# Layer norm on ScalarE, output projection over token tiles of both halves in turn, first FFN pair's second product copied by ScalarE

## The chip, the cores and the metric

One core of a Trainium2 chip runs the kernel. Its engines work side by side, each through its own queue in order: TensorE (PE, matmuls, with PEld for its weight loads), VectorE (DVE), ScalarE (ACT), GpSimd (POOL), and SyncE (SP), which here issues the transfers. Matmul results stand in PSUM, in banks of 128 x 512 float32; everything else on the chip is in SBUF. The metric is the device time of one execution in microseconds (us).

## The reference

A residual stream `x` of 1024 tokens by 1024 goes through two layers. Layer 0 mixes dilated window attention and latent attention, layer 1 is differential attention; both end in an output projection. Then each layer does the same:

```python
x = layer_norm(ALPHA * x + y, ln_mix_g[i], ln_mix_b[i])     # y: output projection of the mixer
f = conv_ffn(x, ffn_w_gate[i], ffn_w_up[i], ffn_conv_w[i], ffn_conv_b[i], ffn_w_down[i])
x = layer_norm(ALPHA * x + f, ln_ffn_g[i], ln_ffn_b[i])
x = x + jax.nn.sigmoid(x @ ple_w_gate[i]) * (p[i] @ ple_w_proj[i])
```

`layer_norm` takes mean and variance over the 1024 columns of a token, and then scales by a gain and adds a bias. `conv_ffn` is a gated FFN of width 2816 with a convolution of three tokens on the gate.

## The kernel before

Tokens lie in eight tiles of 128; the host has put the even tokens into tiles 0 to 3 (the first half) and the odd ones into tiles 4 to 7 (the second half). Every float32 matmul is done as three: each operand is split into a high part (a rounded copy, mostly by ACT or POOL) and a low part (the rest, mostly by DVE), and `mm3` multiplies high by high, high by low and low by high.

**Output projection** (`out_proj`, L1052). For each tile t: SP loads the residual row; `load(t + 1)` fetches and splits the next tile's mixer output (`mhl`); `linear(t)` runs 48 matmuls into a pair of banks, and DVE adds the residual (L1077). Then the tile before is put away (`xt.put(t - 1)`), this one is normed (`ln`), and SP stores it (`xmid`). For the last tile the order is: first FFN weights (`early`), linear, norm, and then the putting away of tile 6; tile 7 is put away by the FFN (`late`). Norm and split of one tile thus stand beside the linear of the next.

**Layer norm** (`LN`, L876) has two parts. `stats`: two `bn_stats` of 512 columns and one `bn_aggr` on DVE, then two small steps on POOL for the reciprocal root (L895, L896). `apply`: DVE subtracts the mean and scales (L901), DVE multiplies by the gain (L902), and POOL adds the bias, or DVE where the argument `last` is true (L903; the last two tiles of an output projection, and all of the embedding stage). The first DVE instruction is pinned: it stays behind all that was written before it for DVE. Other instructions may stand in another order on an engine than in the text; the order is fixed when the kernel is built.

**Splits for the FFN** (`XSeven.put`, L338). The FFN's two products work by a scheme with seven products in place of eight on halves of tokens and halves of the contraction: `b00` and `b10` are the first half's rows, `t1` and `b11` come from the second half with the first half's values subtracted, and `t2`, `t3`, `t4` are made of both at the end (`finish`). PE transposes the tile into two banks; for tiles 0 to 3 ACT copies four high parts and DVE makes four low ones; for tiles 4 to 7 there are twelve operations on DVE and five on ACT, and DVE and ACT take turns on a bank. Tile t of the second half needs tile t - 4.

**FFN** (`ffn`, L1222). For each of 22 weight blocks m, seven products of 12 matmuls, in the order a00, s2, s3, s1, a01, a11, s4. The first pair (m = 0, 1) runs in another order, a00 and a01 first, then s1, s4, s2, s3, a11, since these need the second half later (`go_ahead`, `ahead`). a00 and s2 share a pair of banks (`pa`), of which there are two; the other products take one of four banks (`pb`). `read` adds the products up: `m` is a copy of a00 by ACT, `u2 = m + s2` is one DVE add that reads the bank (through the helper line L1167), and `u3`, `c01` and the rest are built on `u2`.

**Embedding stage** (`Embedding`, L1391). The same `LN` is used on the FFN's result; the norm of tile t + 2 is written ahead of the linear of tile t. The norms of tiles 0 and 1 lie inside the last group of the down projection.

Buffers: 36 units of 4 KB a partition (`unit`) hold rows, weights and splits; `b00` and `b10` take eight of them, the second half's splits twelve.

Of the kernel before, what the change touches and what calls it, by code (L numbers as in the profile page):

```python
# [11 lines left out]
AF = mybir.ActivationFunctionType  # L12
ALU = mybir.AluOpType
AX = mybir.AxisListType

P = 128
NT = 8
# [3 lines left out]
LN_EPS = 1e-5  # L21
# [10 lines left out]
def tile_hybrid_encoder(  # L32
# [32 lines left out]
    nc = tc.nc  # L65
# [8 lines left out]
    def nm(s):  # L74
        count[0] += 1
        return f"{s}_{count[0]}"

    def unit(s, shape, dt=F32):
        return up.tile(shape, dt, tag="u", name=nm(s))
# [29 lines left out]
    def small(s, shape, dt=F32, bufs=6):  # L109
        return sm.tile(shape, dt, tag=s, name=nm(s), bufs=bufs)  # L110
# [4 lines left out]
    def mid2(s, shape, dt=F32):  # L115
        return sm.tile(shape, dt, tag="mid2", name=nm(s), bufs=4)
# [4 lines left out]
    def bank(s):  # L121
        return ps.tile([P, 512], F32, tag="b", name=nm(s), bufs=4)

    def banks2(s):
        return ps.tile([P, 1024], F32, tag="s", name=nm(s), bufs=2)

    def f32(ap):
        return ap.bitcast(F32)
# [28 lines left out]
    def mm3(o, lh, ll, rh, rl, start, stop):  # L157
        nc.tensor.matmul(o, lhsT=lh, rhs=rh, start=start, stop=False)  # L158
        nc.tensor.matmul(o, lhsT=lh, rhs=rl, start=False, stop=False)  # L159
        nc.tensor.matmul(o, lhsT=ll, rhs=rh, start=False, stop=stop)  # L160
# [116 lines left out]
    class XTok:  # L277
# [26 lines left out]
        def load(self, t):  # L304
            self.raw[t] = unit("x0r", [P, NK, P])
            nc.sync.dma_start(out=self.raw[t], in_=xT_in[t])
# [10 lines left out]
    def add(o, a, b, op=ALU.add, eng=None):  # L317
        (eng or nc.vector).tensor_tensor(f32(o), f32(a), f32(b), op=op)
# [557 lines left out]
    class LN:  # L876
# [7 lines left out]
            self.apply(x, self.stats(x), last)  # L884

        def stats(self, x, pin=True):
            st = small("st", [P, 2, 6], bufs=3)
            mv = small("mv", [P, 2], bufs=3)
            rs = small("rs", [P, 1], bufs=3)
            for i in range(2):  # L890
                ins = nc.vector.bn_stats(out=st[:, i, :], in_=x[:, i * 512:i * 512 + 512])
                if pin:
                    tc.keep_in_program_order(ins)
            nc.vector.bn_aggr(out=mv, in_=st)
            nc.gpsimd.tensor_scalar(rs, mv[:, 1:2], 1.0, LN_EPS, op0=ALU.mult, op1=ALU.add)  # L895
            nc.gpsimd.tensor_tensor(rs, rs, mhalf, op=ALU.pow)  # L896
            return mv, rs

        def apply(self, x, stats, last=False):
            mv, rs = stats  # L900
            nc.vector.tensor_scalar(x, x, mv[:, 0:1], rs, op0=ALU.subtract, op1=ALU.mult)  # L901
            nc.vector.tensor_tensor(x, x, self.g, op=ALU.mult)  # L902
            (nc.vector if last else nc.gpsimd).tensor_tensor(x, x, self.b, op=ALU.add)  # L903

# [115 lines left out]
    def mixer_c(xt, late):  # L1020
        new_region(3)
        oT2 = big("oT2", [P, 2, 1024])
        last = {}

        def sink(i):
            def f(oT):
                if i < 7:
                    nc.sync.dma_start(out=mix[1][i], in_=oT)
                last["oT"] = oT
            return f  # L1030
        blk = [Block64(xt, w_c[i], False) for i in range(8)]
        blk[0].load(True)
        for t in range(NT):
            blk[0].project(t, 2)
            if t == 1:
                late()
        blk[0].keys(NT - 2)
        items, plan = [], Plan()
        for i in range(8):
            sti = {"sink": sink(i), "oT": oT2[:, i % 2, :] if i < 7 else unit("oT", [P, 1024])}  # L1040
            items += [ItemC(blk[i], t, sti) for t in range(NT)]
            if i < 7:
                blk[i + 1].plan(plan, 8 * i - 1, 1)
            else:
                w, mt = last_plan(plan, 1, 56, 63)
        plan.add(-1, "first", lambda: blk[0].keys(NT - 1))
        plan.add(-1, "last", lambda: blk[1].load(True), lambda: blk[1].project(0))
        pipeline(items, plan)
        return w, mt, last["oT"]


    def out_proj(i, w, mt, oT, xsrc, xt, early):  # L1052

        ln = LN(ln_mg[i], ln_mb[i])
        xns, m = [], mt.m

        def load(t):
            if t < NT:
                if t not in m:
                    mt.seven(t)  # L1060
                mt.last(t, oT)

        def residual(t):
            xns.append(unit("xn", [P, 1024]))
            nc.sync.dma_start(out=xns[t], in_=xsrc[t])

        def linear(t, beside=None):

            xr, mt_ = xns[t], m.pop(t)
            po = banks2("po")  # L1070
            for k in range(NK):
                if k == NK // 2 and beside:
                    beside()
                for n in range(2):
                    sl = slice(512 * n, 512 * n + 512)
                    mm3(po[:, sl], *mt_[k], w[k][0][:, sl], w[k][1][:, sl], k == 0, k == NK - 1)
            nc.vector.scalar_tensor_tensor(xr, xr, ALPHA, po, op0=ALU.mult, op1=ALU.add)  # L1077

        load(0)
        for t in range(NT):  # L1080
            residual(t)
            load(t + 1)
            if t < NT - 1:
                linear(t)
            else:
                early(0)
                linear(t, lambda: early(1))
                ln(xns[t], True)
                nc.sync.dma_start(out=xmid[i][t], in_=xns[t])
            if t:  # L1090
                xt.put(t - 1, xns[t - 1])
            if t < NT - 1:
                ln(xns[t], t == NT - 2)
                nc.sync.dma_start(out=xmid[i][t], in_=xns[t])
        return lambda: xt.put(NT - 1, xns[NT - 1])


    class Weights:
# [37 lines left out]
    class Products:  # L1136
# [27 lines left out]
        def read(self):  # L1164

            def plus(o, a, name):
                nc.vector.tensor_tensor(o, a, self.o[name], op=ALU.add)  # L1167
            out = []
            had = set(x for x, _ in self.sums)
            for name, need in list(self.sums):  # L1170
                before = {"m": (), "u2": ("m",), "u3": ("u2",), "c11": ("u3",), "c00": ("m",) if self.ahead else ("u2",), "c10": ("u3", "c11"), "k5": (),
                          "c01": ("c11",)}[name]
                if any(x not in self.o for x in need) or any(x in had for x in before):
                    continue
                if name == "m":
                    self.m = mid2("m", [P, 512])
                    nc.scalar.copy(self.m, self.o["a00"])
                elif name == "u2":
                    u = unit("u", [P, 2, 512])
                    self.u2, self.u3 = u[:, 0, :], u[:, 1, :]  # L1180
                    plus(self.u2, self.m, "s2")
                elif name == "u3":
                    plus(self.u3, self.u2, "s3")
                elif name == "k5":
                    self.c11 = mid2("c11", [P, 512])
                    nc.scalar.copy(self.c11, self.o["s1"])
                elif name == "c11" and self.ahead:
                    nc.gpsimd.tensor_tensor(self.u2, self.u2, self.c11, op=ALU.add)
                    nc.vector.tensor_tensor(self.c11, self.u3, self.c11, op=ALU.add)
                elif name == "c11":  # L1190
                    self.c11 = mid2("c11", [P, 512])
                    plus(self.c11, self.u3, "s1")
                    plus(self.u2, self.u2, "s1")
                elif name == "c00":
                    if self.c00 is None:
                        self.c00 = self.m
                    plus(self.c00, self.m, "a01")
                elif name == "c10":
                    plus(self.u3, self.u3, "a11")
                    self.c10 = self.u3  # L1200
                elif name == "c01":
                    plus(self.u2, self.u2, "s4")
                    self.c01 = self.u2
                had.discard(name)
                out.append(name)
            self.sums = [x for x in self.sums if x[0] in had]
            return out
# [254 lines left out]
    xt = XTok()  # L1462
    for i in range(2):
        if i == 0:
            w, mt, oT = mixer_ab(xt)
        else:
            tc.keep_in_program_order(nc.scalar.preload_act_table_set("natural_log_exp_and_others"))
            w, mt, oT = mixer_c(xt, late)
# [3 lines left out]
        if i == 0:  # L1472
            xt = XTok()
# [102 lines left out]
```

## Time and profile before

| | |
|---|---|
| median of 3 runs | 3108.19 us (3105.83 to 3110.84) |
| the profiled execution | 3106.23 us |
| its span | 3104.4 us |
| output projection of layer 0, first to last matmul | 703.2 to 799.6 us |
| its FFN's first product | from 799.5 us |
| last matmul of the output projection of layer 1 | begins at 2314.6 us |
| granted PE clock over the span | 0.994 |

In a row of the profile stand line, engine, operation, output and inputs by name, their shapes, the count, and then busy time and mean of one in ns, and idle time of the engine just before with what ended it (`<-`). A helper's operations all carry the helper's line: L141 is every low part, L1167 every add of `plus`, L163 every transpose. Rows of the order of time have the start and the duration first. A busy PE need not be a PE at its peak: matmuls overlap in the pipeline.

### The profile page before, as it was taken

The page shows a single profiled execution, that of the slowest core. Times are in us where ns is not written, and L with a number is a line of the kernel's source. Part 1 is how long each engine was busy: PE and PEld are TensorE (multiplying, and loading weights), DVE is VectorE, ACT ScalarE, POOL GpSimd, SP SyncE. Part 2 cuts the span into 40 slices and gives each one's busy share as a digit, 9 for nine tenths or more (in the row PEclk, how much of TensorE's full clock was granted, in tenths as well). Part 3 has the DMA queues.
Part 4 walks back from the last instruction along what each step waited for, and adds up shares of the span by engine and source line. Part 5 has one row for each costly group of instructions (what it writes and reads, how often), then busy time and mean ns, then how long its engine had stood idle before and what let it go on. Part 6 is the DMA issues. An engine that isn't in the chain of part 4 may idle for free.

```text
span 3104.4 us, 43067 instructions
## 1 busy us (share of the span) xinstructions
PE 3008.3 (97%) x15720; PEld 2582.7 (83%) x15720; DVE 2280.5 (73%) x3890; ACT 1186.8 (38%) x2538; POOL 1022.9 (33%) x1536
## 2 busy tenths in 40 slices
PE   8999999999899999999999999999998999999999
PEld 7888989887678888888888999998776888878887
DVE  6666487876898887766638777777679888877764
ACT  5555477761232222101225555555413222211111
POOL 4444534333222221101225555554223222211112
PEclk9999999999999999999999999999999999999999
DMA  3000100033222222623111000002431222243321
GB/s 121 28 28 24 33 28 8 25 126 126 85 82 82 82 82 93 220 95 109 55 59 36 32 28 28 28 24 77 156 107 68 82 82 82 82 176 136 103 77 65
DMA packets 89251, 237.52 MB, mean 77 GB/s; under 512 B 9040, under 2 KB 32720, under 8 KB 89040
## 3 DMA queue, kind: packets, MB, share of 16 engines
q1 hardware_dynamic: 89040, 234.76, 22.0%
q8 instruction: 125, 2.05, 0.3%
q14 instruction: 86, 0.70, 0.1%
HBM read 179.15 MB, written 55.57 MB: 76 GB/s over the span
## 4 chain that ended last, share of the span: by engine, by line
PE 79%; DVE 10%; DMA 3%; ACT 2%; issue 2%; POOL 2%; SPq 0%; DVEq 0%; ACTq 0%; POOLq 0%
PE pb L159 6%; PE pb L160 6%; PE pb L158 6%; PE xt L163 5%; PE pd L158 4%; PE pd L159 4%; PE pd L160 4%; PE pp L158 4%; PE pp L160 4%; PE pp L159 4%; PE s L587 4%; PE pa L158 2%; PE pa L160 2%; PE pa L159 2%; PE pg L158 2%
## 5 line engine op out<-in xcount | busy, mean ns | idle before, releaser
L141 DVE TENSOR_TENSOR ptl<-xt,pth 128x512 fp32r<-128x512 f32 (+2 forms) x384 | 239.6, 652 | 60.3 <-ACT pth L398 43.6
L158 PE MATMUL pd<-dh,dh 128*128 128x512 f32 x704 | 274.8, 390 | 3.0 <-DVE xn L1378 2.9
L1378 DVE TENSOR_TENSOR xn<-xn,pd 128x512 f32<-128x512 f32 x320 | 212.5, 683 | 87.9 <-PE pd L160 87.2
L158 PE MATMUL pp<-wh,xth 128*128 128x384 f32 x768 | 266.2, 347 | 9.7 <-ACT wh L145 7.3
L159 PE MATMUL pd<-dl,dh 128*128 128x512 f32 x704 | 274.1, 389 | 0.3 <-DVE dl L141 0.3
L160 PE MATMUL pd<-dh,dl 128*128 128x512 f32 x704 | 273.3, 389 | 0.0
L159 PE MATMUL pp<-wl,xth 128*128 128x384 f32 x768 | 259.0, 337 | 1.9 <-DVE wl L148 1.7
L160 PE MATMUL pp<-wh,xtl 128*128 128x384 f32 x768 | 258.0, 336 | 0.0
L439 ACT ACTIVATE e<-s,nmx 128x1024 f32<-128x1024 f32 x192 | 214.5, 1119 | 81.8 <-DVE nmx L837 59.0
L163 PE MATMUL xt<-ident,e 128*128 128x128 f32 x1440 | 198.8, 275 | 9.9 <-POOL e L739 3.0
L324 ACT CAST w<-ws 128x512 fp32r<-128x512 f32 x132 | 81.3, 621 | 331.6 <-PE pb L160 285.9
L158 PE MATMUL pb<-xt,w 128*128 128x512 f32 x528 | 207.1, 392 | 0.0
L159 PE MATMUL pb<-xt,w 128*128 128x512 f32 x528 | 206.9, 392 | 0.0
L160 PE MATMUL pb<-xt,w 128*128 128x512 f32 x528 | 206.7, 392 | 0.0
L163 PEld LDWEIGHTS xt<-ident,e 128*128 128x128 f32 x1440 | 164.1, 141 | 30.6 <-ACT sq L869 5.8
L138 POOL TENSOR_SCALAR w<-ws 128x512 fp32r<-128x512 f32 x44 | 32.5, 741 | 469.3 <-PE pa L160 419.0
L324 ACT CAST dh<-dr 128x1024 fp32r<-128x1024 f32 x44 | 46.1, 1052 | 335.8 <-DMA dr<-gated 202.1
L141 DVE TENSOR_TENSOR w<-ws,w 128x512 fp32r<-128x512 f32 x176 | 161.0, 918 | 4.5 <-ACT w L324 2.2
L138 POOL TENSOR_SCALAR dh<-dr 128x1024 fp32r<-128x1024 f32 x44 | 46.2, 1052 | 356.1 <-PE pd L159 168.5
L158 PEld LDWEIGHTS pd<-dh,dh 128*128 128x128 f32 x704 | 132.2, 188 | 32.7 <-DVE xn L1378 5.1
L158 PEld LDWEIGHTS pp<-wh,xth 128*128 128x128 f32 x768 | 144.6, 188 | 15.2 <-ACT wh L145 8.1
L159 PEld LDWEIGHTS pd<-dl,dh 128*128 128x128 f32 x704 | 132.2, 188 | 27.7 <-DVE dl L141 0.7
(281 smaller groups left out, 8732.4 us busy)
## 6 DMA issues: line engine op xcount, KB each, us to landing
wf<-in_w_gate_dram SPq DMA_DIRECT2D x44, 512.0 KB, 3.8
wf<-in_w_up_dram SPq DMA_DIRECT2D x44, 512.0 KB, 4.1
gated<-c SPq DMA_DIRECT2D x44, 512.0 KB, 2.8
dr<-in_w_down_dram SPq DMA_DIRECT2D x44, 512.0 KB, 3.2
dr<-gated SPq DMA_DIRECT2D x44, 512.0 KB, 3.5
wr<-in_w_c_dram SPq DMA_DIRECT2D x32, 384.0 KB, 3.3
pes<-peo SPq DMA_DIRECT2D x64, 128.0 KB, 1.9
xmid<-xn SPq DMA_DIRECT2D x16, 512.0 KB, 2.8
```

Source lines behind the costliest of these rows:

```text
L138: nc.gpsimd.tensor_scalar(o, i, 1.0, 1.0, op0=ALU.mult, op1=ALU.mult)
L141: nc.vector.tensor_tensor(lo, src, f32(hi), op=ALU.subtract)
L158: nc.tensor.matmul(o, lhsT=lh, rhs=rh, start=start, stop=False)
L159: nc.tensor.matmul(o, lhsT=lh, rhs=rl, start=False, stop=False)
L160: nc.tensor.matmul(o, lhsT=ll, rhs=rh, start=False, stop=stop)
L163: nc.tensor.transpose(o, in_=i, identity=ident)
L324: nc.scalar.copy(h, v)
L439: nc.scalar.activation(dst, s, AF.Exp, bias=negmax, scale=1.0, accum_out=l)
L587: nc.tensor.matmul(s[:, kh * 512:kh * 512 + 512], lhsT=qt[:, hl, i, :], rhs=self.ks[kh][:, j, :], start=hl == 0, stop=hl == 1)
L1378: nc.vector.tensor_tensor(xns[t][:, sl], xns[t][:, sl], po, op=ALU.add)
```

## The change

Layer norm: the sum over a row comes from an ACT copy in place with its accumulator (pinned on ACT); POOL makes minus the mean over 32; two ACT squares of 512 columns, with that as bias and a scale of 1/32, write to a PSUM bank that nobody reads and give the variance by their accumulators; POOL takes two small steps to the reciprocal root and a third to mean times root; ACT scales and shifts the row. DVE keeps the multiplication by the gain, and POOL or DVE the bias as before.

Output projection: the tiles come in the order 0, 4, 1, 5, 2, 6, 3, 7.

FFN, first pair only: ACT copies s2 out of its bank, and DVE adds `m` to it in SBUF.

```diff
--- before.py
+++ after.py
@@ -884,21 +884,24 @@
             self.apply(x, self.stats(x), last)
 
         def stats(self, x, pin=True):
-            st = small("st", [P, 2, 6], bufs=3)
-            mv = small("mv", [P, 2], bufs=3)
-            rs = small("rs", [P, 1], bufs=3)
+
+            st = small("st", [P, 6], bufs=3)
+            sums, sq, nm, rs, nmr = st[:, 0:1], st[:, 1:3], st[:, 3:4], st[:, 4:5], st[:, 5:6]
+            ins = nc.scalar.activation(x, x, AF.Identity, accum_out=sums)
+            if pin:
+                tc.keep_in_program_order(ins)
+            nc.gpsimd.tensor_scalar(nm, sums, -1.0 / (1024 * 32), 1.0, op0=ALU.mult, op1=ALU.mult)
             for i in range(2):
-                ins = nc.vector.bn_stats(out=st[:, i, :], in_=x[:, i * 512:i * 512 + 512])
-                if pin:
-                    tc.keep_in_program_order(ins)
-            nc.vector.bn_aggr(out=mv, in_=st)
-            nc.gpsimd.tensor_scalar(rs, mv[:, 1:2], 1.0, LN_EPS, op0=ALU.mult, op1=ALU.add)
+                nc.scalar.activation(bank("sq"), x[:, i * 512:i * 512 + 512], AF.Square, bias=nm, scale=1.0 / 32,
+                                     accum_out=sq[:, i:i + 1])
+            nc.gpsimd.tensor_scalar(rs, sq[:, 0:1], sq[:, 1:2], LN_EPS, op0=ALU.add, op1=ALU.add)
             nc.gpsimd.tensor_tensor(rs, rs, mhalf, op=ALU.pow)
-            return mv, rs
+            nc.gpsimd.tensor_scalar(nmr, rs, nm, 32.0, op0=ALU.mult, op1=ALU.mult)
+            return nmr, rs
 
         def apply(self, x, stats, last=False):
-            mv, rs = stats
-            nc.vector.tensor_scalar(x, x, mv[:, 0:1], rs, op0=ALU.subtract, op1=ALU.mult)
+            nmr, rs = stats
+            nc.scalar.activation(x, x, AF.Identity, bias=nmr, scale=rs)
             nc.vector.tensor_tensor(x, x, self.g, op=ALU.mult)
             (nc.vector if last else nc.gpsimd).tensor_tensor(x, x, self.b, op=ALU.add)
 
@@ -1052,16 +1055,18 @@
     def out_proj(i, w, mt, oT, xsrc, xt, early):
 
         ln = LN(ln_mg[i], ln_mb[i])
-        xns, m = [], mt.m
-
-        def load(t):
-            if t < NT:
+        xns, m = {}, mt.m
+        turn = [4 * (n % 2) + n // 2 for n in range(NT)]
+
+        def load(n):
+            if n < NT:
+                t = turn[n]
                 if t not in m:
                     mt.seven(t)
                 mt.last(t, oT)
 
         def residual(t):
-            xns.append(unit("xn", [P, 1024]))
+            xns[t] = unit("xn", [P, 1024])
             nc.sync.dma_start(out=xns[t], in_=xsrc[t])
 
         def linear(t, beside=None):
@@ -1077,22 +1082,22 @@
             nc.vector.scalar_tensor_tensor(xr, xr, ALPHA, po, op0=ALU.mult, op1=ALU.add)
 
         load(0)
-        for t in range(NT):
+        for n, t in enumerate(turn):
             residual(t)
-            load(t + 1)
-            if t < NT - 1:
+            load(n + 1)
+            if n < NT - 1:
                 linear(t)
             else:
                 early(0)
                 linear(t, lambda: early(1))
                 ln(xns[t], True)
                 nc.sync.dma_start(out=xmid[i][t], in_=xns[t])
-            if t:
-                xt.put(t - 1, xns[t - 1])
-            if t < NT - 1:
-                ln(xns[t], t == NT - 2)
+            if n:
+                xt.put(turn[n - 1], xns[turn[n - 1]])
+            if n < NT - 1:
+                ln(xns[t], n == NT - 2)
                 nc.sync.dma_start(out=xmid[i][t], in_=xns[t])
-        return lambda: xt.put(NT - 1, xns[NT - 1])
+        return lambda: xt.put(turn[-1], xns[turn[-1]])
 
 
     class Weights:
@@ -1178,7 +1183,11 @@
                 elif name == "u2":
                     u = unit("u", [P, 2, 512])
                     self.u2, self.u3 = u[:, 0, :], u[:, 1, :]
-                    plus(self.u2, self.m, "s2")
+                    if self.ahead:
+                        nc.scalar.copy(self.u2, self.o["s2"])
+                        add(self.u2, self.u2, self.m)
+                    else:
+                        plus(self.u2, self.m, "s2")
                 elif name == "u3":
                     plus(self.u3, self.u2, "s3")
                 elif name == "k5":
```

## The prediction

> **What bounds the kernel now.** I read the page first, then the busy time by stretches, then the list of who waited for whom, and at last the order of instructions where PE waits.
>
> ```profile
> span 3104.4 us, 43067 instructions
> ...
> PE 3008.3 (97%) x15720; PEld 2582.7 (83%) x15720; DVE 2280.5 (73%) x3890; ACT 1186.8 (38%) x2538; POOL 1022.9 (33%) x1536
> ```
>
> PE stands idle for 3104.4 - 3008.3 = 96.1 us in all. Work taken off another engine can only win where PE waits for that engine, so the question is where the 96 us lie. These are stretches of the first layer, one row that the second layer gives for the same place, and one of the embedding stage (us, then busy time and count of PE, PEld, DVE, ACT, POOL, granted clock, DMA):
>
> ```profile
> core 0: us, PE busy (x) PEld busy (x) DVE busy (x) ACT busy (x) POOL busy (x), PEclk, DMA share, GB/s
> ...
> 800.00:848.00 48.00, 36.84 (x159) 28.83 (x157) 44.82 (x67) 16.31 (x28) 13.25 (x11) 0.93 0.19 66
> 848.00:860.00 12.00, 10.72 (x36) 8.43 (x37) 11.42 (x17) 5.36 (x7) 3.26 (x3) 0.71 0.00 1
> 860.00:896.00 36.00, 33.40 (x146) 26.84 (x145) 35.71 (x51) 11.73 (x17) 13.53 (x12) 1.00 0.29 100
> 896.00:1240.00 344.00, 344.00 (x1504) 280.66 (x1503) 275.17 (x390) 100.18 (x143) 88.46 (x85) 1.00 0.23 83
> 1480.00:1560.00 80.00, 79.91 (x396) 66.62 (x395) 54.48 (x79) 18.61 (x34) 17.82 (x23) 1.00 0.17 60
> 2315.00:2411.00 96.00, 81.36 (x340) 64.52 (x339) 91.98 (x132) 33.45 (x51) 30.00 (x25) 0.93 0.20 70
> ```
>
> From 800 to 896 us, the turn from the output projection to the FFN, DVE is busy 44.82 + 11.42 + 35.71 = 91.95 of 96 us and PE 80.96; the second layer has 91.98 and 81.36. After 896 PE is never idle (344 of 344, 344 / 1504 = 0.229 us a matmul), and so it is in the embedding stage (79.91 of 80). So two stretches of 96 us are DVE's, and nearly all the rest in reach of this change is PE's. PE's waits over the whole span say the same:
>
> ```profile
> PE pa L158 <- DVE u L1167: 18.3, 2, 9.2
> ...
> PE xt L163 <- POOL xn L903: 4.9, 4, 1.8
> PE pb L158 <- DVE t L318: 4.0, 2, 2.0
> ...
> PE pb L158 <- DVE u L1167: 2.8, 2, 1.4
> ...
> PE xt L163 <- DVE xn L903: 2.4, 4, 0.7
> PE pa L158 <- ACT m L1177: 2.2, 2, 1.2
> ```
>
> They come to 34.6 us, 17.3 a layer. Slow matmuls after the longest wait cost more: 848 to 860 has 36 in 10.72 us, 10.72 - 36 x 0.229 = 2.5 us too long, at a clock of 0.71. So about 20 us a layer, 40 in all, is the ceiling of this change.
>
> **Layer norm, off DVE.** The prices on DVE and POOL now:
>
> ```profile
> L891 DVE BATCH_NORM_STATS2 st<-xn 128x6 f32<-128x512 f32 x64 | 41.4, 680 | 0.2
> ...
> L902 DVE TENSOR_TENSOR xn<-xn,lngb 128x1024 f32<-128x1024 f32 x32 | 39.1, 1222 | 0.6
> ...
> L901 DVE TENSOR_SCALAR xn<-xn,mv,rs 128x1024 f32<-128x1024 f32 x32 | 26.6, 831 | 26.0 <-POOL rs L896 26.0
> L894 DVE BATCH_NORM_AGGREGATE mv<-st 128x2 f32<-128x12 f32 x2 | 0.4, 190 | 0.0
> L903 POOL TENSOR_TENSOR xn<-xn,lngb 128x1024 f32<-128x1024 f32 x12 | 29.5, 2458 | 26.7 <-DVE xn L902 26.7
> ...
> L896 POOL TENSOR_TENSOR rs<-rs,mhalf 128x1 f32<-128x1 f32 x32 | 17.5, 548 | 2.7
> L895 POOL TENSOR_SCALAR rs<-mv 128x1 f32<-128x1 f32 x32 | 8.0, 248 | 156.7 <-DVE mv L894 156.1
> ```
>
> DVE loses 2 x 0.68 + 0.19 + 0.83 = 2.38 us a token tile, 76 us over 32 tiles. Of these only the tiles normed inside the DVE-bound stretch count: the last two of each output projection, 4.8 us a layer. ACT takes the work over; these are the nearest rows:
>
> ```profile
> L439 ACT ACTIVATE e<-s,nmx 128x1024 f32<-128x1024 f32 x192 | 214.5, 1119 | 81.8 <-DVE nmx L837 59.0 <-DVE nmx L735 22.6
> ...
> L324 ACT CAST w<-ws 128x512 fp32r<-128x512 f32 x132 | 81.3, 621 | 331.6 <-PE pb L160 285.9 <-DVE c L1242 33.4 <-DVE ws L318 10.8
> ...
> L324 ACT CAST dh<-dr 128x1024 fp32r<-128x1024 f32 x44 | 46.1, 1052 | 335.8 <-DMA dr<-gated 202.1 <-DVE xn L1378 113.4 <-PE pd L160 15.7
> ...
> L439 ACT ACTIVATION_READ_ACCUMULATOR e<-s,nmx 128x1 f32 x192 | 37.5, 195 | 0.0
> ...
> L1234 ACT ACTIVATE c<-c,convt 128x512 f32<-128x512 f32 x24 | 19.6, 816 | 92.6 <-DVE c L1167 74.9 <-DVE c L1189 11.2 <-DVE xt L141 6.6
> ```
>
> The sum: 1.05 to 1.12 plus a read of 0.20. Two squares of 512: between the plain 0.62 and 0.82 (bias and scale both from a tile), I take 0.7 for the single bias, plus 0.20 each: 1.8. The scaling, 1024 elements with both: 0.82 + (1.05 - 0.62) = 1.25. ACT gains 4.3 us a tile; at 16.31 busy of 48 it has room. The chain from residual to normed row is now 2 x 0.68 + 0.19 + 0.25 + 0.55 + 0.83 = 3.2 us before the multiply by the gain. After: 1.3 + 0.25 (mean) + 1.8 + 0.25 + 0.55 + 0.25 (three POOL steps) + 1.25 = 5.65, and two more changes of engine. I take **2.5 us longer**; the bounds are 2.0 (squares at 0.62, steps hidden) and 3.5 (POOL steps stretched beside DVE).
>
> On this cost the Trainium skill bears (ScalarE: Activation LUTs, Rules for kernel authors): adds and multiplies belong on VectorE and not on ScalarE. The trace agrees on the single price, 0.83 us on DVE against 1.05 for a plain pass on ACT; by that rule alone the edit would only lengthen the chain, which is the last rival below.
>
> **What the longer chain meets.** The splits of tiles 3, 4 and 5 in the first output projection begin at these transposes (PE), and the norms of tiles 4 and 5 at these statistics (DVE); the last row is the end of tile 4's norm (POOL):
>
> ```profile
> 762.15 1.03 PE L163 MATMUL xt<-ident,xn 128*128 128x128 f32 x8
> 773.93 1.04 PE L163 MATMUL xt<-ident,xn 128*128 128x128 f32 x8
> 787.85 1.09 PE L163 MATMUL xt<-ident,xn 128*128 128x128 f32 x8 [1.76 <-POOL xn L903]
> ```
>
> ```profile
> 765.02 1.28 DVE L891 BATCH_NORM_STATS2 st<-xn 128x6 f32<-128x512 f32 x2
> ...
> 780.09 1.28 DVE L891 BATCH_NORM_STATS2 st<-xn 128x6 f32<-128x512 f32 x2
> ```
>
> ```profile
> 769.64 2.41 POOL L903 TENSOR_TENSOR xn<-xn,lngb 128x1024 f32<-128x1024 f32 x1 [2.19 <-DVE xn L902]
> ```
>
> The statistics are pinned behind the split of the tile before, which waits for that tile's norm: a loop. For a tile of the first half (light split) it runs 762.15 to 769.64 + 2.41 = 772.05, 9.9 us; for one of the second half (heavy split) 773.93 to 787.85, 13.9. PE's own period is 773.93 - 762.15 = 11.8. So a light loop has 1.9 us to spare and a heavy one makes PE wait. With 2.5 more, less some 0.4 and 1.1 because the sum now follows ACT's last copy and not DVE's last operation behind it, a light loop takes 12.0 and a heavy one 15.3 or a little less. In turn 0, 4, 1, 5, 2, 6, 3, 7 three heavy loops lie in the projection (before: two), each 2.5 to 3.5 late, and the waits of 4.9 + 2.4 become about 3 us more a layer: the last linear ends some **2.6 us later**.
>
> **Token tiles in turn.** The price of one operation of a split, from DVE's groups of 786 to 896 us:
>
> ```profile
> L318 DVE TENSOR_TENSOR t<-xt,t 128x256 f32<-128x256 f32 x6 | 2.5, 411 | 0.0
> ```
>
> A heavy split has 12 such operations, 4.9 us; a light one 4, 1.7. Before, tiles 5, 6 and 7 are split after 786 us; after the change 6, 3 and 7. DVE is spared 4.9 - 1.7 = **3.2 us** a layer there, and the heavy ones go to where DVE has room. The price: the first FFN product reads the first half's rows and now needs tile 3, the last but one, where before it needed nothing but weights. PE then waits some 3 us after the last linear; those four products before hid a later wait, so I put this at nothing, up to 3 if DVE isn't ahead by then. Loads and stores only change order; the twelve buffers of the second half are taken three tiles sooner, so SP's loads of the next tile wait for a buffer that the middle of each linear gives back, half a period of 11.8 us ahead of need.
>
> **The first pair's copy.** This is the longest wait:
>
> ```profile
> 849.28 0.77 PE L158 MATMUL pa<-xb,w 128*128 128x512 f32 x1 [9.17 <-DVE u L1167]
> ```
>
> ```profile
> 845.93 1.28 DVE L141 TENSOR_TENSOR w<-wf,w 128x512 fp32r<-128x512 f32 x2
> ...
> 848.45 1.28 DVE L1167 TENSOR_TENSOR u<-m,pa 128x512 f32<-128x512 f32 x2
> ```
>
> PE stops because the bank of the second product is read at 848.45 only. ACT could read it some 10 us sooner. But the weights that PE needs next are split by DVE until 847.2, and the next two products want banks that still wait for DVE's add into u3. So alone this frees 849.28 - 847.2 = 2 us a layer at most; DVE's own add stays (0.68 us). I count 0.5, since it decides only where DVE has come first.
>
> On the slow matmuls the Trainium skill says (TensorE: Matmul & The Clock Gate, Part 1) that an idle window of about 3.4 us halves the clock and a busy one restores it. The clock of 0.71 after 9.17 us agrees; by that rule the 2.5 us come back whole if the wait falls under 3.4.
>
> **The sum.** DVE is spared 4.8 + 3.2 = 8.0 us a layer in the stretch that it bounds. The last norm, from which the heavy split of tile 7 and all of the second half follow, comes later. Now:
>
> ```profile
> 799.24 0.39 PE L160 MATMUL po<-woh,mhl 128*128 128x512 f32 x1
> ```
>
> ```profile
> 801.74 1.20 DVE L1077 SCALAR_TENSOR_TENSOR xn<-xn,po 128x1024 f32<-128x1024 f32 x1
> ...
> 808.66 1.22 DVE L903 TENSOR_TENSOR xn<-xn,lngb 128x1024 f32<-128x1024 f32 x1
> ```
>
> From the last linear's end at 799.63 to the norm's end at 809.88 are 10.25 us, though its parts need 1.20 + 3.2 + 2 x 1.22 = 6.85: 3.4 us are DVE's queue. After, the linear is 2.6 later and the chain 2.5 longer, but most of that queue is gone: about 2 us later. 8.0 - 2.0 + 0.5 = 6.5 us a layer, 13 in all, where DVE fills the 2 us with weight splits. The embedding's norms have 79.91 of 80 busy on PE over them and are due two tiles ahead: nothing, unless ACT's sigmoid is held behind a norm. The profiled execution took 3106.23 us, 1.8 over its span: 3106.2 - 13 = 3093.2. The median of the runs shown is 2.0 above it, so I name **3095**.
>
> **Rivals and chances.** A measurement of this kernel can tell 0.2%, 6 us, from no change: 3102 to 3114.4.
> - Forecast, 0.37: 4 to 9 us a layer, 3088 to 3100.
> - DVE is far enough ahead that the long wait goes with its slow matmuls, 0.16: 9 to 17 a layer, 3072 to 3088. For it: 9.17 + 2.5 hang on one read. Against: from 860 to 896 DVE is busy 35.71 of 36 and would bind again.
> - The longer chain and the wait for tile 3 use up the gain, or the copy changes nothing since DVE's queue sets the order, 0.24: 3100 to 3114, of which 0.05 below 3102.
> - Slower, 0.23: the loop of split and norm becomes the bound of the projection. Seven loops; the gain of 6.5 is gone when each takes 0.9 us more than I sum (POOL's three steps beside DVE, ACT's copies between the parts of a norm). At 1.8 more each the last norm is 12.6 later: +6.1 a layer, 3118. For it: 12.0 and 15.3 already exceed 11.8. Against: PE can run the next linear while a split waits.
>
> Chances: faster 0.37 + 0.16 + 0.05 = 0.58, same 0.19, slower 0.23. The range 3080 to 3118 leaves out half of the second case and half of the last, 0.2 together.
>
> **What would show it.** Right: DVE's busy time 76 us lower and ACT's 137 higher; the read of the second product on ACT; PE's 9.17 us wait shorter by 5 or more; waits of xt for xn longer. Wrong: the last linear of the first layer over 6 us after 799.63; PE idle in the embedding stage; the stretch of DVE's saturation ending no sooner than 896 plus that delay.

## The result, and the profile after

The changed kernel takes 3134.93 us (median of 4 runs, 3133.11 to 3137.62), the kernel before 3107.16 in the same runs: a ratio of 1.0088, with a 95% interval of 1.0071 to 1.0106. It is **slower by 27.8 us**; the forecast of 3095 was wrong in sign, and the range ended at 3118. The changed kernel's page, span and busy times:

```profile
span 3131.3 us, 43231 instructions
...
PE 3015.2 (96%) x15720; PEld 2589.8 (83%) x15720; DVE 2213.3 (71%) x3762; ACT 1311.0 (42%) x2766; POOL 1053.9 (34%) x1600
```

The work went where the diff sends it: DVE is busy 67 us less, ACT 124 more. PE's idle time rose from 96.1 us to 116.1; the rest of the longer span is 6.9 us more of busy time, with the same matmuls. Who waits, in the changed kernel (PE's waits: total, times, longest):

```profile
PE xt L163 <- POOL xn L906: 13.8, 8, 3.0
PE pg L158 <- ACT sg L1455: 11.1, 11, 1.4
PE pa L158 <- ACT xb L358: 11.1, 2, 5.6
PE xt L163 <- DVE xn L906: 10.3, 2, 5.3
...
PE pa L158 <- ACT u L1187: 7.8, 2, 3.9
```

The waits for a normed row (`xn`) grew from 7.3 us to 24.1. Two waits are new: the sigmoid's (`sg`, embedding stage) and that of a00 for tile 3's split (`xb`). The old 18.3 for the first pair's second product fell to 7.8, but the new wait for `xb`, ahead of the same products, is about as long as what fell away.

To place the loss I read the start of the first matmul of each stage from the order of time, and E, the end of the last norm of an output projection (tile 7's bias add on DVE). In the changed kernel, from the first `po` to E takes 118.9 us in layer 0 (before: 106.7) and 120.6 in layer 1 (110.4). From E to the first matmul of the down projection, `pd`, it takes 431.3 (435.2) and 432.0 (435.0). So the projections end 12.2 and 10.2 later, and 3.9 and 3.0 come back: 15.5 us. From the embedding's first matmul to the next stage are 105.9 us (101.6) in layer 0, and 108.3 to the end of the span (101.3) in layer 1: 11.2 us more. 15.5 + 11.2 = 26.7 of the 26.9 by which the span grew; the other stages differ by at most 1.6 either way and nearly cancel.

**The projection of layer 0.** Windows of the kernel before and of the changed one, from the first `po` to the last linear's end, then three short windows of the changed one around its waits, and two around the same waits in layer 1 (us, busy time and count of PE, PEld, DVE, ACT, POOL, granted clock, DMA):

```profile
703.16:799.63 96.47, 93.71 (x433) 77.02 (x434) 63.12 (x111) 12.72 (x35) 30.43 (x37) 1.00 0.38 126
```

```profile
704.72:808.77 104.05, 97.25 (x433) 78.84 (x432) 50.30 (x90) 38.21 (x84) 33.16 (x49) 0.97 0.35 117
...
752.00:758.00 6.00, 3.03 (x14) 2.57 (x14) 3.36 (x6) 2.08 (x5) 2.34 (x1) 0.83 0.49 176
758.00:768.00 10.00, 10.00 (x42) 8.15 (x41) 2.59 (x4) 3.41 (x8) 5.09 (x7) 0.93 0.16 48
...
780.00:786.00 6.00, 3.48 (x14) 2.90 (x14) 3.06 (x6) 1.93 (x5) 2.35 (x1) 0.77 0.39 134
...
2279.80:2285.80 6.00, 3.03 (x18) 2.62 (x18) 3.39 (x6) 2.08 (x5) 2.34 (x1) 1.00 0.47 173
...
2307.00:2313.00 6.00, 3.46 (x20) 2.84 (x20) 3.17 (x6) 2.38 (x6) 2.56 (x2) 1.00 0.41 145
```

PE's idle time grew from 2.76 us to 6.80, and its matmuls became slower: 433 took 93.71 us before and take 97.25 now, at a mean clock of 0.97; 3.5 us went to the clock. The order of time of the changed kernel shows the transposes that begin each split, with what PE waited for:

```profile
739.82 1.09 PE L163 MATMUL xt<-ident,xn 128*128 128x128 f32 x8 [0.91 <-POOL xn L906]
755.03 1.11 PE L163 MATMUL xt<-ident,xn 128*128 128x128 f32 x8 [2.97 <-POOL xn L906]
768.26 1.04 PE L163 MATMUL xt<-ident,xn 128*128 128x128 f32 x8
782.71 1.47 PE L163 MATMUL xt<-ident,xn 128*128 128x128 f32 x8 [2.52 <-POOL xn L906]
796.75 1.09 PE L163 MATMUL xt<-ident,xn 128*128 128x128 f32 x8 [0.40 <-POOL xn L906]
813.78 1.75 PE L163 MATMUL xt<-ident,xn 128*128 128x128 f32 x8 [5.02 <-DVE xn L906]
```

The tiles are 4, 1, 5, 2, 6, 3. Each long wait follows a heavy split (of 4, 5 and 6): 2.97, 2.52 and 5.02; after a light one (of 0, 1 and 2) PE waits 0.91, 0 and 0.40. Up to the last linear's end four waits come to 6.8 us. The kernel before has 0.28 near the start, 1.76 at 787.85 and this one:

```profile
750.28 1.10 PE L163 MATMUL xt<-ident,xn 128*128 128x128 f32 x8 [0.71 <-POOL xn L903]
```

So it is 4.0 more, and with the 3.5 of the clock 7.6. The last matmul of the projection in the changed kernel agrees:

```profile
808.38 0.39 PE L160 MATMUL po<-woh,mhl 128*128 128x512 f32 x1
```

It ends at 808.77, 104.05 us after the first `po`, and 96.47 before: 7.6 later. In layer 1 it is 5.2 later (105.47 us against 100.30): the waits grow by 4.6 there, and after two of the same length, 2.97 and 2.54, the clock stayed at 1.00. A light loop of the changed kernel, from the transposes at 755.03, has these POOL rows, the mean's step and the norm's end:

```profile
758.55 0.19 POOL L893 TENSOR_SCALAR st<-st 128x1 f32<-128x1 f32 x1 [3.58 <-ACT xn L890]
...
765.40 2.41 POOL L906 TENSOR_TENSOR xn<-xn,lngb 128x1024 f32<-128x1024 f32 x1 [1.81 <-DVE xn L905]
```

The loop takes 767.81 - 755.03 = 12.8 us, over PE's period of 11.8. Then the last norm of the changed kernel, on all engines; the first row is the end of tile 3's norm:

```profile
812.43 1.21 DVE L906 TENSOR_TENSOR xn<-xn,lngb 128x1024 f32<-128x1024 f32 x1
813.56 1.21 DVE L1082 SCALAR_TENSOR_TENSOR xn<-xn,po 128x1024 f32<-128x1024 f32 x1
...
814.80 1.06 ACT L890 ACTIVATE xn<-xn 128x1024 f32<-128x1024 f32 x1 [2.77 <-DVE xn L1082]
...
815.77 0.19 ACT L890 ACTIVATION_READ_ACCUMULATOR xn<-xn 128x1 f32 x1
816.04 0.59 POOL L893 TENSOR_SCALAR st<-st 128x1 f32<-128x1 f32 x1 [5.81 <-ACT xn L890]
...
819.63 1.24 ACT L904 ACTIVATE xn<-xn,st 128x1024 f32<-128x1024 f32 x1 [1.46 <-POOL st L899]
...
822.38 1.22 DVE L906 TENSOR_TENSOR xn<-xn,lngb 128x1024 f32<-128x1024 f32 x1
```

From residual add to E it takes 823.60 - 813.56 = 10.0 us, against 809.88 - 801.74 = 8.1 before. The add itself begins 4.8 us after the last matmul's end, right behind tile 3's norm; before, 2.1. So E's 12.2 us are 7.6 + 2.7 + 1.9; in layer 1 they are 5.2 + 3.1 + 1.9. From the last linear's end to E, before and after:

```profile
799.63:809.88 10.25, 9.05 (x43) 6.97 (x42) 9.59 (x16) 1.85 (x4) 0.74 (x2) 1.00 0.13 53
```

```profile
808.77:823.60 14.83, 4.17 (x14) 3.15 (x15) 10.20 (x13) 7.60 (x14) 3.08 (x7) 0.68 0.09 35
```

DVE, the third engine of a row, stood idle for 0.66 us there before and for 4.63 after: it was spared the norm and then waited for it.

**The embedding stage.** The changed kernel on ACT and PE, and the kernel before on ACT:

```profile
1514.82 1.24 ACT L904 ACTIVATE xn<-xn,st 128x1024 f32<-128x1024 f32 x1 [1.44 <-POOL st L899]
1515.96 0.57 ACT L1455 ACTIVATE sg<-pg 128x512 f32<-128x512 f32 x1
...
1516.59 0.50 PE L158 MATMUL pg<-wgh,xth 128*128 128x512 f32 x1 [1.40 <-ACT sg L1455]
```

```profile
1500.88 0.60 ACT L1446 ACTIVATE sg<-pg 128x512 f32<-128x512 f32 x1 [5.64 <-PE pg L160]
...
1512.82 0.60 ACT L1446 ACTIVATE sg<-pg 128x512 f32<-128x512 f32 x1 [4.37 <-PE pg L160]
```

Before, ACT waited for PE ahead of each sigmoid. Now the scaling of a later tile's norm stands ahead of the sigmoid on ACT's queue; ACT idles 1.44 us for POOL's steps with the sigmoid behind it, and PE waits for the bank that the sigmoid reads. Loads of activation tables (`ACT_TABLE_LOAD`, 1.28 us each) are no cause: the traces of both kernels have eight.

### The profile page after: what moved, and what is told of

The parts are those of the page before. It is cut to its first block, busy times and chain, and to the rows that moved or that the text cites. A ratio compares the mean times of both kernels' runs of the same rounds, so it can differ in the third digit from the quotient of the medians.

```text
span 3131.3 us, 43231 instructions
## 1 busy us (share of the span) xinstructions
PE 3015.2 (96%) x15720; PEld 2589.8 (83%) x15720; DVE 2213.3 (71%) x3762; ACT 1311.0 (42%) x2766; POOL 1053.9 (34%) x1600
## 4 chain that ended last, share of the span: by engine, by line
PE 77%; DVE 9%; ACT 4%; DMA 4%; POOL 3%; issue 2%; SPq 0%; DVEq 0%; POOLq 0%; ACTq 0%
PE pb L158 6%; PE pb L160 6%; PE pb L159 6%; PE pd L158 5%; PE pd L159 5%; PE pd L160 5%; PE xt L163 4%; PE pp L158 4%; PE pp L160 4%; PE pp L159 4%; PE s L587 4%; PE pa L158 3%; PE pa L160 2%; PE pa L159 2%; PE av L447 2%
## 5 line engine op out<-in xcount | busy, mean ns | idle before, releaser
L163 PE MATMUL xt<-ident,e 128*128 128x128 f32 x1440 | 198.8, 275 | 10.2 <-POOL e L739 3.0
```

Of the source, the lines that this page charges most:

```text
L163: nc.tensor.transpose(o, in_=i, identity=ident)
```

## The experiments

Each kernel was timed beside the kernel before on the same chip; a ratio is to that, with its 95% interval. The table has the kernels that change the output projection, in us: from the first `po` to E, and from E to the first `pd`, for layers 0 and 1.

| kernel | ratio | po to E | E to pd |
|---|---|---|---|
| before | 1 | 106.7, 110.4 | 435.2, 435.0 |
| before, norm written ahead | 1.001 | 108.0, 108.5 | 437.3, 436.9 |
| turn alone | 1.0015 | 111.7, 116.5 | 431.8, 431.0 |
| other order of tiles, and copy | 0.9985 | 107.4, 110.9 | 433.9, 432.6 |
| the same, ACT norm for two tiles | 1.0008 | 109.6, 113.6 | 432.8, 433.3 |
| ACT norm alone | 1.0069 | 113.1, 116.1 | 434.2, 433.4 |
| ACT norm written ahead, old order of tiles | 1.0039 | 112.9, 115.8 | 435.6, 435.2 |
| changed kernel | 1.0088 | 118.9, 120.6 | 431.3, 432.0 |
| changed, embedding on DVE | 1.0055 | 117.7, 123.2 | 432.2, 432.8 |
| the same, norm written ahead | 1.0060 | 118.7, 122.9 | 431.8, 431.7 |
| before, delay in every norm | 1.0107 | 119.1, 125.2 | 435.8, 437.2 |
| before, delay in the last norm | 1.0017 | 109.3, 112.4 | 435.8, 436.2 |

### The copy alone

```diff
-                    plus(self.u2, self.m, "s2")
+                    if self.ahead:
+                        nc.scalar.copy(self.u2, self.o["s2"])
+                        add(self.u2, self.u2, self.m)
+                    else:
+                        plus(self.u2, self.m, "s2")
```

> Kernel before with the copy of the second product by ScalarE alone. Loop theory (the changed kernel lost its time because split and norm of successive token tiles form a loop, which the norm on ScalarE makes longer than PE's period) and buffer theory (it lost it because the second half's buffers are taken three tiles sooner) agree here: 0 to -5 us against before, since PE's wait of 9.2 us a layer is shared by the weight splits behind it. If the copy itself were harmful: over +3.

Measured: 3106.06 us against 3107.48, ratio 0.9998 (0.9988 to 1.0007): nothing. ACT in the kernel with the copy alone:

```profile
847.86 0.62 ACT L324 CAST w<-ws 128x512 fp32r<-128x512 f32 x1 [2.81 <-DVE ws L318]
848.38 1.07 ACT L1182 COPY u<-pa 128x512 f32<-128x512 f32 x2
```

The copy stands on ACT's queue behind a weight cast that waits for DVE. It begins at 848.38; DVE's own read began at 848.45. The read moved to another engine and not in time.

### The turn alone

```diff
+        turn = [4 * (n % 2) + n // 2 for n in range(NT)]
...
-        for t in range(NT):
+        for n, t in enumerate(turn):
```

> Kernel before with the token tiles in turn alone; norm on DVE. Loop theory: light loops of 9.9 us fit PE's 11.8, three heavy ones of 13.9 cost 2 us each, and DVE is spared 3.2 us after the projection: -4 to +6 us against before. Buffer theory: next tiles' loads and splits wait for buffers as in the changed kernel, +12 to +25 us.

Measured: 3111.7 us, ratio 1.0015 (1.0005 to 1.0024), by which it is +4.6; far from the 12 to 25 that the buffers, taken sooner, were to cost. The norms are DVE's as before. PE's transposes for tile 3 in this kernel:

```profile
807.97 1.30 PE L163 MATMUL xt<-ident,xn 128*128 128x128 f32 x8 [4.55 <-DVE xn L903]
```

The table has the two sides: 3.3 and 4.0 us are won behind E, which agrees with the 3.2 of the splits that moved, and E is 5.0 and 6.1 later.

### The ACT norm alone

The new `stats` and `apply` of the change as they are, in the old order of tiles and without the copy, in both stages:

```diff
-            mv, rs = stats
-            nc.vector.tensor_scalar(x, x, mv[:, 0:1], rs, op0=ALU.subtract, op1=ALU.mult)
+            nmr, rs = stats
+            nc.scalar.activation(x, x, AF.Identity, bias=nmr, scale=rs)
```

> Kernel before with layer norm on ScalarE alone, both stages; tiles in their old order. Loop theory: light loops just reach PE's period, the heavy ones at the end exceed it, and in the embedding stage the sigmoid waits behind a norm (+5 a layer): +8 to +25 us against before, PE's waits of xt for xn over 10 us in all. Buffer theory: only the embedding's part, +8 to +12, with waits of xt for xn as before (7 us).

Measured: 3127.7 us, ratio 1.0069 (1.0054 to 1.0084), +20. PE's waits for `xn` come to 14.7 us, where the buffers' theory had 7. By the table E is 6.4 and 5.7 later and 1.0 and 1.6 come back: 9.5. The rest is the embedding stage, where `pg` waits for `sg` as in the changed kernel. So the norm carries some 20 of the 27.8, and the turn 5 to 7.

### The changed kernel with the embedding's norms on DVE

`LN` is the old norm again; the new one, as `LNA`, is used in `out_proj` only.

```diff
-        ln = LN(ln_mg[i], ln_mb[i])
+        ln = LNA(ln_mg[i], ln_mb[i])
```

> The changed kernel, with the embedding stage's norms back on DVE. Between the projection's first matmul in the second layer and the end the changed kernel lost 6 to 7 us in the second embedding stage and about 5 in the first: 9 to 13 us faster than the changed kernel, 3122 to 3126, if the sigmoid behind the norm is the cause there; no more than 3 us faster if the shifted start of the FFN is.

Measured: 3123.69 us, ratio 1.0055 (1.004 to 1.007): 11 less than the changed kernel.

### The changed kernel with the embedding's norms written later

```diff
                 if n == 0:
                     self.turn(t + 1)
+                    self.norm(t + 2)
...
-                self.norm(t + 2)
                 self.linear(t)
```

> The changed kernel, with the embedding's norm of the tile after next written behind the first half's sigmoid and the next tile's split, in place of ahead of the linear. If the sigmoid stuck behind the norm's last pass is what the embedding loses: PE's waits of pg for the sigmoid (11.1 us) fall below 3 and the time by 6 to 11 us, to 3124 to 3129. If it is ScalarE's load or the bank that the squares take: within 3 us of 3135.

Measured: 3125.28 us, ratio 1.0055 (1.004 to 1.007): 9.7 less, with all of the norm still on ACT, and the wait of `pg` for `sg` is gone from PE's waits. The embedding's two stretches take 101.4 and 100.3 us again. Its 11 us are thus the place of the norm on ACT's queue and not ACT's load.

### A delay in every norm of the projection

```diff
-            self.apply(x, self.stats(x), last)
+            stats = self.stats(x)
+            for _ in range(4):
+                nc.gpsimd.tensor_tensor(stats[1], stats[1], ones[:, 0:1], op=ALU.pow)
+            self.apply(x, stats, last)
```

The powers by 1 leave the result as it is.

> Kernel before (norm on VectorE, old order) with four powers with exponent 1 added on POOL to the reciprocal root in the projection: the chain of each norm is 2.6 us longer, as with ScalarE, but no engine on PE's way has more work. Loop theory: +8 to +13 us, what layer norm on ScalarE costs in the projections of both layers (3128 less 11 for the embedding, less 3107.5). Rival, ScalarE's queue and load: at most +4.

Measured: 3139.64 us, ratio 1.0107 (1.009 to 1.0124), **+32**: about three times the loop theory's 8 to 13, and eight times its rival's 4. Neither had the size. PE's waits in this kernel:

```profile
PE xt L163 <- POOL xn L906: 18.3, 9, 4.3
...
PE xt L163 <- DVE xn L906: 6.5, 4, 2.8
```

24.8 us of waits for `xn`, as in the changed kernel (24.1), with nothing moved to ACT and nothing in another order. Latency in the norm is enough. A delay of 2.43 us put E 12.4 later in layer 0, about five times its size: the waits up to the last linear's end grew by 5.5, the matmuls took 3.4 longer, and from there to E it takes 3.6 more. Why the ACT norm alone, whose chain is longer by about 2 us, put E only 6.4 and 5.7 later isn't shown; it also takes 2.38 us a tile off DVE.

### The norm ahead of the split, changed kernel and kernel before

```diff
-            if n:
-                xt.put(turn[n - 1], xns[turn[n - 1]])
             if n < NT - 1:
                 ln(xns[t], n == NT - 2)
                 nc.sync.dma_start(out=xmid[i][t], in_=xns[t])
+            if n:
+                xt.put(turn[n - 1], xns[turn[n - 1]])
```

> The run with the embedding's norms on VectorE (3124 us), with one change: in the projection the norm of a tile is written ahead of the split of the tile before, so that the pinned sum no longer stands behind that split's copies. Loop theory: the loop is cut and the norm has 10.7 us for a period of 11.8; PE's waits of transposes for normed rows (22 us in all) fall below 8 and the time by 6 to 14 us, to 3110 to 3118. Rival, the load: ScalarE's and POOL's added work or the buffers taken sooner hold PE, whatever the order: within 3 us of 3124.

> Kernel before with that change of order alone (norm ahead of the split of the tile before, on VectorE). Loop theory: its two heavy loops a layer, which cost PE some 3.6 us a layer, go: -1 to -6 us against before. Rival: no loop binds before, and the split that now stands behind the norm is late instead: 0 to +5.

Measured: 3126.82 us (the embedding's norms are on DVE here, so the mate is the 3123.69), ratio 1.006 (1.0045 to 1.0075); and 3110.17, ratio 1.001 (1.0 to 1.0019). Neither is a gain. PE's waits in the first of the two:

```profile
PE pa L158 <- ACT xb L358: 14.7, 2, 7.4
PE po L160 <- DVE mhl L148: 9.4, 6, 2.4
...
PE po L158 <- POOL mhl L138: 6.7, 2, 3.6
```

The waits for `xn` are gone from the list's head, so the loop was cut. In their place PE waits 16.1 us for the next tile's mixer splits, and a00 longer for tile 3.

### The same without the turn

```diff
-        turn = [4 * (n % 2) + n // 2 for n in range(NT)]
...
-        for n, t in enumerate(turn):
+        for t in range(NT):
```

That is the first kernel of the last pair, with the tiles in their old order.

> The changed kernel with the token tiles in their old order, with each norm written ahead of the previous tile's split, and with the embedding's norms on VectorE: the run with the swapped order (3126.8 us) without the turn. Theory A (there the loop was cut, and the second half's splits, waiting for mixer buffers that the turn takes sooner, had become the bound: 16 us of waits of po for mhl): those waits fall below 4 us and the time to 3108 to 3116. Theory B (the longer chain of the norms in the projection costs its 10 us in any order of tiles and writing): 3115 to 3121, with pa no earlier than 806 us of the span in the first layer.

Measured: 3119.83 us, ratio 1.0039 (1.0024 to 1.0053). The waits of `po` for `mhl` fall to 4.6, so the turn had a part in them, and the first FFN product begins at 800.1, nearly as early as before, where the other theory had 806 or later. But the time stays within that theory's 3115 to 3121: E is still 6.2 and 5.4 later than before. In layer 0 the last linear ends 97.5 us after the first `po` (the ACT norm alone: 101.2, before: 96.5), so most of what the loops cost is back; 5.2 of the 6.2 lie between that end and E. One row carries 1.8 of them:

```profile
806.35 2.40 POOL L914 TENSOR_SCALAR st<-st 128x1 f32<-128x1 f32 x1 [7.33 <-ACT xn L911]
```

POOL's mean, one column, took 2.40 us inside the last norm, while DVE was splitting weights; the same step had taken 0.59 in the changed kernel. In layer 1 the last linear is still 3.0 late, 2.2 of it in slower matmuls.

### Another order of tiles, and the ACT norm where DVE is full

```diff
-        turn = [4 * (n % 2) + n // 2 for n in range(NT)]
+        turn = [0, 1, 4, 2, 5, 3, 6, 7]
```

With the copy and the DVE norm; the second kernel has the ACT norm for tiles 6 and 7 of each projection.

> The kernel before, with the copy of the first pair's second product and with the tiles of both halves mixed in the order 0, 1, 4, 2, 5, 3, 6, 7; the norm stays on VectorE. Tile 3 is now put away two tiles before the end, so the first FFN product needs nothing late, as in the kernel before. Theory A (the turn by itself cost 4.6 us because a00 waits for tile 3's split behind the last linear, 8.5 us a layer, of which the FFN head gave 6.8 back): the first pa starts at about 800 us of the span and VectorE's spared 2 to 3 us a layer show as time: 4 to 8 us below the kernel before, 3099 to 3104. Theory B (the turn costs because the second half's buffers are taken sooner and the heavy splits stand close together, whatever the first product waits for): 0 to 6 us above, 3107 to 3114, with the last linear no earlier than in the turn-only run. A waits row of pa for ACT's xb under 1 us speaks for A, one over 3 us against it.

> The run with the order 0, 1, 4, 2, 5, 3, 6, 7, and the ScalarE norm for the last two tiles of each output projection only (6 and 7); the other tiles and the embedding keep VectorE's norm. Theory A (what VectorE gets back counts only where VectorE is full, and there it is worth its 4.8 us a layer less the longer chain of the last norm, 2.5 us): 2 to 6 us below that run. Theory B (the end of the projection is set by the chain of the last norms, not by VectorE's load: the run with a delay of 2.43 us a norm lost 32 us): 2 to 8 us above that run, the put of tile 7 later by 3 to 5 us a layer.

Measured: 3103.91 us, ratio **0.9985** (0.9976 to 0.9994), 4.3 below the kernel before: the one version that beats both, by little. The transposes for tile 3 and, after the last linear, for tile 6 in this kernel:

```profile
788.19 1.09 PE L163 MATMUL xt<-ident,xn 128*128 128x128 f32 x8 [1.84 <-POOL xn L903]
...
800.04 1.03 PE L163 MATMUL xt<-ident,xn 128*128 128x128 f32 x8
```

Tile 3 is put away a tile earlier, and a00, from 800.8, no longer waits for it. E is 0.7 and 0.5 later, and 1.3 and 2.4 come back. With the ACT norm for the last two tiles it takes 3111.34, ratio 1.0008 (0.9999 to 1.0018), 7.4 more: E is 2.2 and 2.7 later again, and of this nearly nothing comes back. Even where DVE is full, taking the norm off it at the price of a longer chain lost.

### A delay in the last norm alone

The four powers by 1 of above, here for tile 7 only.

```diff
-                ln(xns[t], True)
+                ln(xns[t], True, 4)
```

> The kernel before, with four powers by 1 on GpSimd (the result is unchanged) in the last norm of each output projection only, tile 7's, 2.4 us longer; the other norms are as they were. Theory A (in the runs so far the FFN's second stage begins 431 to 437 us after the end of that norm, whatever came ahead of it, so a later end moves all that follows one for one): 2 to 3 us a layer, 4 to 6 us in all, 3111 to 3114, and still 435 us from the norm's end to the first pd. Theory B (the 96 us behind the norm are bound by VectorE's load, which is unchanged; the 32 us of the run with a delay in every norm came from the loops ahead): 0 to 1.5 us in all, and about 433 us from the norm's end to the first pd.

Measured: 3114.47 us, ratio 1.0017 (1.0008 to 1.0026), by which it is +5.3 for 2 x 2.43 us. The kernel with this delay, in order of time:

```profile
805.60 2.43 POOL L886 TENSOR_TENSOR rs<-rs,ones 128x1 f32<-128x1 f32 x4
...
810.60 1.22 DVE L906 TENSOR_TENSOR xn<-xn,lngb 128x1024 f32<-128x1024 f32 x1
```

E is at 811.82, and `pd` begins 435.8 us behind it. What comes after the last norm moves with it one for one.

## Why the prediction was wrong

**"Two stretches of 96 us are DVE's".** This is the step from which the sign came. The stretch has two parts that the prediction took as one. From E on it is DVE's: the 3.2 us of splits that the turn takes away from there came back (3.3 and 4.0). The ten microseconds ahead of E are the norm's chain, and DVE's work was counted there as though less of it made the whole shorter. The delay in the last norm alone shows that E sets when the rest begins: nothing was added to DVE, and all of the delay was paid. Within a layer, over the table's twelve kernels, E to `pd` varies by 6 us, `po` to E by 12 to 17. A busy share near 1 over both parts was read as one bound. No run takes work off DVE ahead of E without a longer chain, so what that alone is worth is not shown.

**"DVE is spared 4.8 + 3.2 = 8.0 us a layer".** The 3.2 of the moved splits was right. The 4.8 of the norms lies ahead of E, where DVE then stood idle (4.63 us), and the ACT norm alone gave 1.0 and 1.6 behind E. In the changed kernel 3.9 and 3.0 came back, not 8.0.

**"The last linear ends some 2.6 us later".** It was 7.6 in layer 0 and 5.2 in layer 1. The loops themselves were sized well: "a heavy one 15.3", "each 2.5 to 3.5 late", and the trace has 15.2 from 739.82 to 755.03 and waits of 2.97 and 2.52, with 5.02 for the third, behind the last linear; the light loop, 12.0 in the text, took 12.8. The sum made of them failed. Three loops at 3 us are 9, and the text sets them against "4.9 + 2.4", which are the waits of both layers and not of one. And the clock was left out: 3.5 us in layer 0, about 0.5 in layer 1.

On the clock the Trainium skill says (TensorE: Matmul & The Clock Gate, Part 1) that an idle window of about 3.4 us halves it. Here PE's waits of 2.97 and 2.52 us in layer 0 left granted clocks of 0.83 and 0.77 in windows of 6 us, and those of 2.97 and 2.54 in layer 1 left 1.00, as did 0.71 and 1.76 in the kernel before. In the turn alone 2.06 us in layer 1 left 0.83. By the measurement, waits shorter than the page's window can cost clock, and their length alone doesn't tell which do.

**"Most of that queue is gone: about 2 us later".** In layer 0 the norm was 1.9 longer from add to end, near the 2.5 of the text. But the wait ahead of the residual add grew from 2.1 to 4.8 us: the last operation of tile 3's norm, late itself, stood there on DVE's queue. E was 12.2 later and not 2.

**"I put this at nothing, up to 3".** a00's wait for tile 3 was 5.6 us a layer. Whether it cost time is not shown: it ends before E (821.18 against 823.60), and with it the part from E to `pd` is among the shortest. The order that puts tile 3 away earlier takes 3103.91, where the turn alone took 3111.7, but that order also puts tile 6 behind tile 3, and much of its gain lies ahead of E (107.4 against 111.7).

**"ACT could read it some 10 us sooner", counted 0.5.** The copy alone changed nothing, so the small price was near. The reason was not: ACT was not free to read sooner, it stood behind a cast.

**"Nothing, unless ACT's sigmoid is held behind a norm".** It was held, and the embedding took 11.2 us longer in all. The condition was named and not worked out: on a queue in order, a chain of seven ACT instructions with two pauses for POOL holds whatever is written after it.

**The rivals.** The last one, slower by the loop of split and norm, had the mechanism, with 0.23 and a price of 3118 (+6.1 a layer). Its "last norm is 12.6 later" came close (12.2 and 10.2). Measured were 8.3 and 7.2 a layer, and the embedding's 11.2 came on top. Two of the text's own signs of being wrong came too: a last linear over 6 us late (7.6 in layer 0), and PE idle in the embedding stage. By the Trainium skill's rule (ScalarE: Activation LUTs, Rules for kernel authors) adds and multiplies stay on VectorE; the ACT norm alone, 1.0069, agrees in sign here, though about half of its 20 us is the norm's place on ACT's queue. The delay alone, 1.0107, says that latency suffices for a loss in the projection.

What stays open is why writing the norm ahead of the split returns so little. In layer 0 the loops' cost came back and a later last norm took its place; 1.8 us of that is a POOL step of 2.40 us, which was not taken away by itself.

## What to carry to other kernels

Before work is taken off a busy engine, find the event from which its busy stretch begins, and ask which of the work taken off lies behind that event: here only that part came back, and delaying the event alone by two microseconds moved all that follows. In a loop that several tiles run one after another, a longer chain is paid in each loop that has no slack, and sometimes again through the clock. A chain that pauses for another engine holds everything written behind it on its own queue, so where it is written matters as much as what it costs.

## What the runs showed of the hardware

POOL's mean, a step on one column, took 0.19 us in the light loop, 0.59 in the changed kernel's last norm and 2.40 once, the last two beside DVE's splits of weights. An ACT sum over a row costs its pass of 1.06 us and a separate read of the accumulator of 0.19. PE waits of 2.5 to 3.0 us were followed by granted clocks of 0.77 to 0.83 in layer 0, and 0.93 in the ten microseconds after one of them; waits of the same length in layer 1 of the same kernel left 1.00.
